# Hybrid decoder trunk: vector products of the mixer moved to GpSimd and ScalarE, one small matmul group moved by a unit

## The chip, the cores and the metric

The kernel runs on one core of a Trainium2 chip. The metric is the device time of one execution in microseconds (us), lower is better; the number compared is the median of the runs.

## The reference

The reference is a decoder trunk of two layers on 256 tokens with 1024 channels, all in float32. Each layer is a feed-forward block, a mixer and a second feed-forward block, each with an RMS norm ahead of it and added to the residual. The mixer is what the change touches:

```
h = rms_norm(x)                      # 256 x 1024
one projection h @ w_in -> columns of three causal attentions:
  A stick-breaking (4 heads)
  B NSA (8 query heads, 2 key/value groups): compressed, selected-block and sliding-window branches
      q = rope(rms_norm(q, q_norm));  k_cmp = rope(rms_norm(silu(flat @ w1) @ w2, k_norm))
  C DSA (4 query heads, one shared key head): indexer scores -> top 64 keys -> softmax
      q = rope(rms_norm(q, q_norm));  k = rope(rms_norm(k, k_norm))
merged = sum over b of sigmoid(h @ w_gate)_b * (o_b @ w_br_b);   x = x + merged @ w_out
```

Each head of 64 numbers is normed by itself: it is multiplied by its reciprocal root mean square and then by a vector of norm weights, and the first 16 numbers are rotated (rope).

## The kernel before

**Weights.** Every weight matrix is streamed from HBM in tiles `raw` of 128x1024 numbers and used in one pass. Each number is split into a high part (`wh`, rounded to the fast float32 form that TensorE takes) and the rest (`wl`): ScalarE makes `wh` by a copy (L242), VectorE makes `wl` by a subtraction (L244). One such tile with its matmuls is called a **unit** (`unit`, `run_unit`). There are three buffers for `wh` and for `wl` and four for `raw`; the split runs two units ahead of the matmuls (`LA = 2`).

**Order of the work.** TensorE's instructions stand in exactly the order of the program text: each matmul is tied behind the one before it. Around the units stand `threads`: Python generators (`keys`, `queries`, `compress`, `indexer`, `dsa`, `nsa_units` and others). After every unit `tick()` lets each thread whose wait has run out go on to its next `yield n`, which means "n units later". So a `yield` decides behind which unit a thread's matmuls stand. On the other engines a scheduler sets the order within each queue, and each queue is then run strictly in order.

**The mixer's units.** `ORDER` lists the column groups: group 0, the compressed keys' columns `f`, group 3, gate tile 0, group 4 (the NSA queries), gate tile 1, group 1 (stick-breaking), group 2, and then the ten other gate tiles. A result collects in one of three PSUM banks `acc` and must be read out ("evacuated") before the bank is used again; transposes go through two PSUM banks `tp`. `evens` (L631 on) sends evacuations to ScalarE and VectorE in turn.

**What the change touches.**
- `gate_rows` (L618 on): evacuates a finished gate bank (128x512) on VectorE, multiplied by the token norm `R`, into `gl`. The sigmoid that reads `gl` comes at the end of the mixer.
- `norm_rope` (L668 on): squares, sums, reciprocal root, product with the root (L676), product with the norm weights `hg` (L679), then `rope` (L648 to L652). It is called for the DSA heads and keys (`p1`, 9 heads) and for the two token halves of the NSA queries (`q8[0]`, `q8[1]`, 8 heads each). The page calls all of these tiles `p` or `q`.
- `keys`: splits the keys into high and low parts (`kk`, `kc`), transposes them, and evacuates the transposed DSA key as `kD` by `evens`: one token half on ScalarE (L635), the other on VectorE (L637). Then the DSA queries (`dq`, evacuated as `qD`).
- `compress`: first layer, `silu` and the second layer of the compressed keys. `hrep` is the input of the second layer and `c2s` its result; `kc` from `c2s` is transposed later and evacuated as `kC`.
- `queries`: after `norm_rope`, ScalarE makes the high part of the queries (L880) and VectorE the low part (L881).

The steps in `compress` and `queries` read:

```python
            yield 2
            c2 = hid[:, S + P:2 * S]
            for kv in range(2):
                mm(c2[:, kv * HD:(kv + 1) * HD], hrep[:, kv].rearrange("p i g c -> p (i g c)"), w2[:, kv], True, True)
...
            for t in range(NT):
                A.activation(out=q8[t][:, :, 0:HD].bitcast(F32R), in_=q8[t][:, :, HD:P], func=AF.Copy)
                V.tensor_tensor(out=q8[t][:, :, HD:P], in0=q8[t][:, :, HD:P], in1=q8[t][:, :, 0:HD], op=ALU.subtract)
```

Of the kernel before, what the change touches and what calls it, by code (L numbers as in the profile page):

```python
# [13 lines left out]
AF = mybir.ActivationFunctionType  # L14
ALU = mybir.AluOpType
AX = mybir.AxisListType

P = 128
D = 1024
S = 256  # L20
# [5 lines left out]
HD = 64  # L26
# [97 lines left out]
def decoder_trunk(ctx: ExitStack, tc: tile.TileContext, x_in, consts, gains, hgain, gu1, dn1, win, wkc, wgate, cw1, cw2,  # L124
                  cpe, wbr, wout, gu2, dn2, out, depth=DEPTH):
    nc = tc.nc
    V, A, G, T = nc.vector, nc.scalar, nc.gpsimd, nc.tensor
# [78 lines left out]
    def spawn(gen, wait=1):  # L206
        threads.append([gen, wait])
# [282 lines left out]
    def mixer(l, nrm, nxt):  # L490
# [127 lines left out]
        def gate_rows(n, a):  # L618
            def f(_):
                if a == 0:  # L620
                    return
                if n % 2 == 0:
                    gl[n // 2] = b4("gl")
                V.tensor_tensor(out=gl[n // 2][:, (n % 2) * 512:(n % 2 + 1) * 512].rearrange("p (a b) -> p a b", b=S),
                                in0=gb[n].rearrange("p (a b) -> p a b", b=S),
                                in1=N["R"].unsqueeze(1).to_broadcast([P, 2, S]), op=ALU.mult)
            return f

        turn = [0]

        def evens(out, in_):  # L631

            turn[0] ^= 1
            if turn[0]:
                A.activation(out=out, in_=in_, func=AF.Copy)  # L635
            else:
                V.tensor_copy(out=out, in_=in_)  # L637
# [28 lines left out]
        def norm_rope(v, nh, gs, t0=0):  # L666
# [10 lines left out]
            for a, n, k in gs:  # L677
                g = hg[:, k * HD:(k + 1) * HD].unsqueeze(1).unsqueeze(1)
                V.tensor_tensor(out=v[:, :, a:a + n], in0=v[:, :, a:a + n], in1=g.to_broadcast([P, nt, n, HD]),  # L679
                                op=ALU.mult)  # L680
# [91 lines left out]
        def keys():  # L772
            yield from need(0, 3)
            yield from norm_rope(p1, 9, ((0, 4, 0), (4, 1, 1), (5, 2, 2), (7, 2, 4)))
            for t in range(NT):
# [10 lines left out]
                tp = transposes([k1[:, 0, 0:P], k1[:, 0, P:256]])  # L786
                evens(out=kD[:, :, s], in_=heads(tp))
            dq = b4("dq").rearrange("p (t h a d) -> p t h a d", t=NT, a=2, d=HD)
# [14 lines left out]
        def compress():  # L803
# [36 lines left out]
            for kv in range(2):  # L840
                a, b = (v[:, kv * 2 * NC:(kv + 1) * 2 * NC].rearrange("p (g c) -> p g c", c=NC).unsqueeze(1)
                        .to_broadcast([P, 4, 2, NC]) for v in (hs, tp))
                V.tensor_tensor(out=hrep[:, kv, :, :, 0:NC], in0=b, in1=a, op=ALU.mult)
            yield 2
            c2 = hid[:, S + P:2 * S]
# [27 lines left out]
        def queries():  # L873
# [5 lines left out]
            for t in range(NT):  # L879
                A.activation(out=q8[t][:, :, 0:HD].bitcast(F32R), in_=q8[t][:, :, HD:P], func=AF.Copy)  # L880
                V.tensor_tensor(out=q8[t][:, :, HD:P], in0=q8[t][:, :, HD:P], in1=q8[t][:, :, 0:HD], op=ALU.subtract)  # L881
            yield 2
# [384 lines left out]
```

## Time and profile before

| what | value |
|---|---|
| median of 3 runs | 1208.97 us (1208.77 to 1208.98) |
| the profiled execution's own time | 1211.23 us |
| span of its trace, first to last instruction | 1209.5 us |
| TensorE busy | 1197.8 us, 99% of the span |
| VectorE busy | 884.2 us, 73% |
| ScalarE busy | 697.9 us, 58% |
| GpSimd busy | 145.8 us, 12% |
| granted TensorE clock | 1.00 in every slice, which is the 2.4 GHz level |

The engines are called PE (TensorE, its weight loads PEld), DVE (VectorE), ACT (ScalarE), POOL (GpSimd) and SP in the profile. A share over the whole span is an average over stages: the feed-forward blocks fill most of it, and the two mixers lie at about 200 to 395 us and 797 to 1000 us. Where TensorE is nearly always busy, the time follows from the few places where it isn't, and from what ends the wait there.

### The profile page before, as it was taken

The page shows a single profiled execution, that of the slowest core. Times are in us where ns is not written, and L with a number is a line of the kernel's source. Part 1 is how long each engine was busy: PE and PEld are TensorE (multiplying, and loading weights), DVE is VectorE, ACT ScalarE, POOL GpSimd, SP SyncE. Part 2 cuts the span into 40 slices and gives each one's busy share as a digit, 9 for nine tenths or more (in the row PEclk, how much of TensorE's full clock was granted, in tenths as well). Part 3 has the DMA queues.
Part 4 walks back from the last instruction along what each step waited for, and adds up shares of the span by engine and source line. Part 5 has one row for each costly group of instructions (what it writes and reads, how often), then busy time and mean ns, then how long its engine had stood idle before and what let it go on. Part 6 is the DMA issues. An engine that isn't in the chain of part 4 may idle for free. (4 is left out here: it accounts for less than half of the span.)

```text
span 1209.5 us, 20859 instructions
## 1 busy us (share of the span) xinstructions
PE 1197.8 (99%) x7878; PEld 1070.7 (89%) x7878; DVE 884.2 (73%) x1577; ACT 697.9 (58%) x1261; POOL 145.8 (12%) x181
## 2 busy tenths in 40 slices
PE   8999999999999999999999999999999999999998
PEld 7888888879999988888888888898898999888887
DVE  7766677897766877776777666788977587876664
ACT  6655555565675565555555555555666745655542
POOL 2211011220000111110111110112100001111100
PEclk9999999999999999999999999999999999999999
DMA  7555566644334555556656555666533345555563
GB/s 263 187 185 184 179 190 200 216 152 136 122 95 152 180 189 190 190 187 190 191 181 192 189 182 184 188 188 219 166 123 113 106 155 187 191 192 192 183 200 106
DMA packets 60885, 212.09 MB, mean 175 GB/s; under 512 B 6992, under 2 KB 8048, under 8 KB 60784
## 3 DMA queue, kind: packets, MB, share of 16 engines
q1 hardware_dynamic: 60192, 209.65, 54.2%
q0 software_dynamic: 448, 1.08, 0.4%
q8 instruction: 62, 1.02, 0.3%
q14 instruction: 39, 0.32, 0.1%
q10 hardware_dynamic: 144, 0.02, 0.0%
HBM read 209.15 MB, written 1.05 MB: 174 GB/s over the span
## 5 line engine op out<-in xcount | busy, mean ns | idle before, releaser
L242 ACT ACTIVATE wh<-raw 128x1024 fp32r<-128x1024 f32 (+4 forms) x402 | 412.2, 1028 | 401.8 <-PE acc L196 277.8
L244 DVE TENSOR_TENSOR wl<-raw,wh 128x1024 fp32r<-128x1024 f32 (+4 forms) x400 | 473.9, 1187 | 211.5 <-ACT wh L242 210.6
L196 PE MATMUL acc<-aT,wh 128*128 128x512 f32 (+1 forms) x1696 | 415.1, 343 | 1.3 <-ACT wh L242 1.3
L196 PEld LDWEIGHTS acc<-aT,wh 128*128 128x128 f32 x1696 | 265.0, 189 | 41.9 <-ACT wh L242 1.7
L196 PE MATMUL acc<-aT,wl 128*128 128x256 f32 x1280 | 297.9, 281 | 1.2 <-DVE wl L244 1.2
L196 PE MATMUL acc<-hT,wh 128*128 128x512 f32 (+1 forms) x792 | 236.2, 367 | 0.0
L196 PEld LDWEIGHTS acc<-aT,wl 128*128 128x128 f32 x1280 | 216.1, 190 | 3.7 <-DVE wl L244 2.8
L196 PE MATMUL sc<-aT,wh 128*128 128x512 f32 x544 | 191.7, 396 | 0.0
L196 PE MATMUL acc<-hT,wl 128*128 128x256 f32 x704 | 184.5, 280 | 0.0
L196 PEld LDWEIGHTS acc<-hT,wh 128*128 128x128 f32 x792 | 137.2, 188 | 25.8
L196 PE MATMUL sc<-aT,wl 128*128 128x256 f32 x544 | 151.1, 279 | 0.0
L196 PEld LDWEIGHTS acc<-hT,wl 128*128 128x128 f32 x704 | 126.8, 188 | 0.0
L196 PEld LDWEIGHTS sc<-aT,wh 128*128 128x128 f32 x544 | 101.8, 188 | 24.0
L442 POOL TENSOR_TENSOR v<-v,R 128x256 f32<-128x256 f32 x88 | 70.6, 806 | 412.3 <-DVE v L358 359.2
L196 PEld LDWEIGHTS sc<-aT,wl 128*128 128x128 f32 x544 | 102.4, 188 | 0.4
L386 POOL TENSOR_TENSOR ssum<-ssum,sq 128x256 f32<-128x256 f32 x42 | 38.3, 912 | 445.5 <-ACT sq L385 445.3
L196 PE MATMUL acc<-wh,aT 128*128 128x512 f32 (+1 forms) x320 | 81.1, 394 | 0.2
L196 PEld LDWEIGHTS acc<-wh,aT 128*128 128x128 f32 x320 | 57.5, 188 | 11.0 <-ACT p L526 1.1
L357 ACT ACTIVATE half<-acc 128x256 f32<-128x256 f32 x136 | 49.5, 366 | 3.7 <-PE acc L196 3.2
L444 DVE TENSOR_TENSOR v<-v,v 128x256 f32<-128x256 f32 x88 | 38.2, 436 | 13.3 <-ACT v L443 5.8
L358 DVE TENSOR_TENSOR v<-acc,half 128x256 f32<-128x256 f32 x108 | 44.7, 417 | 1.5 <-ACT half L357 1.5
L376 DVE SCALAR_TENSOR_TENSOR aT<-x,gn,aT 128x256 fp32r<-128x256 f32 x48 | 40.6, 856 | 7.0 <-ACT aT L375 7.0
(239 smaller groups left out, 1217.2 us busy)
## 6 DMA issues: line engine op xcount, KB each, us to landing
raw<-in_gu SPq DMA_DIRECT2D x175, 512.0 KB, 4.0
raw<-in_dn SPq DMA_DIRECT2D x64, 512.0 KB, 3.7
raw<-in_wgate SPq DMA_DIRECT2D x48, 512.0 KB, 3.6
raw<-in_win SPq DMA_DIRECT2D x32, 512.0 KB, 3.7
raw<-in_dn SPq DMA_DIRECT2D x32, 384.0 KB, 3.0
raw<-in_wbr SPq DMA_DIRECT2D x16, 512.0 KB, 3.5
raw<-in_wout SPq DMA_DIRECT2D x16, 512.0 KB, 3.5
raw<-in_cw SPq DMA_DIRECT2D x8, 512.0 KB, 4.4
```

Of the source, the lines that this page charges most:

```text
L196: return pe(T.matmul(o, lhsT=lhsT, rhs=rhs, start=start, stop=stop, skip_group_check=True))
L242: A.activation(out=wh[:, w], in_=raw[:, w], func=AF.Copy)
L244: e.tensor_tensor(out=wl[:, w], in0=raw[:, w], in1=wh[:, w].bitcast(F32), op=ALU.subtract)
L357: A.activation(out=t, in_=b[:, S:2 * S], func=AF.Copy)
L358: V.tensor_tensor(out=o, in0=b[:, 0:S], in1=t, op=ALU.add)
L376: V.scalar_tensor_tensor(out=dst[:, m, 1], in0=xs[m], scalar=g[:, m:m + 1], in1=dst[:, m, 0].bitcast(F32), op0=ALU.mult, op1=ALU.subtract)
L386: G.tensor_tensor(out=ssum, in0=ssum, in1=sq, op=ALU.add)
L442: G.tensor_tensor(out=g, in0=g, in1=N["R"], op=ALU.mult)
L444: V.tensor_tensor(out=u, in0=u, in1=g, op=ALU.mult)
```

## The change

Five edits, all in the mixer, so each is made once in each of the two layers:
1. Gate tiles 0 and 1 are evacuated by ScalarE as a plain copy; their product with `R` is made by GpSimd in place, spawned for 22 units later. The ten others stay as they were.
2. The product with the norm weights goes to GpSimd for the NSA queries (8 heads); the 9 heads of `p1` stay on VectorE.
3. Both halves of `kD` are evacuated by ScalarE.
4. The second compression layer stands three units behind the first layer's last step in place of two, and what follows it in `compress` moves with it.
5. The low part of the NSA queries is made by GpSimd.

```diff
@@ gate_rows
-                V.tensor_tensor(out=gl[n // 2][:, (n % 2) * 512:(n % 2 + 1) * 512].rearrange("p (a b) -> p a b", b=S),
-                                in0=gb[n].rearrange("p (a b) -> p a b", b=S),
-                                in1=N["R"].unsqueeze(1).to_broadcast([P, 2, S]), op=ALU.mult)
+                g = gl[n // 2][:, (n % 2) * 512:(n % 2 + 1) * 512].rearrange("p (a b) -> p a b", b=S)
+                b = gb[n].rearrange("p (a b) -> p a b", b=S)
+                r = N["R"].unsqueeze(1).to_broadcast([P, 2, S])
+                if n < 2:
+
+                    A.activation(out=g, in_=b, func=AF.Copy)
+                    spawn(scaled(g, r), 22)
+                else:
+                    V.tensor_tensor(out=g, in0=b, in1=r, op=ALU.mult)
             return f
+
+        def scaled(g, r):
+            G.tensor_tensor(out=g, in0=g, in1=r, op=ALU.mult)
+            yield 1
@@ norm_rope
-                V.tensor_tensor(out=v[:, :, a:a + n], in0=v[:, :, a:a + n], in1=g.to_broadcast([P, nt, n, HD]),
+                e = G if nh == 8 else V
+                e.tensor_tensor(out=v[:, :, a:a + n], in0=v[:, :, a:a + n], in1=g.to_broadcast([P, nt, n, HD]),
                                 op=ALU.mult)
@@ keys
-                evens(out=kD[:, :, s], in_=heads(tp))
+                A.activation(out=kD[:, :, s], in_=heads(tp), func=AF.Copy)
@@ compress
-            yield 2
+            yield 3
             c2 = hid[:, S + P:2 * S]
@@ queries
-                V.tensor_tensor(out=q8[t][:, :, HD:P], in0=q8[t][:, :, HD:P], in1=q8[t][:, :, 0:HD], op=ALU.subtract)
+                G.tensor_tensor(out=q8[t][:, :, HD:P], in0=q8[t][:, :, HD:P], in1=q8[t][:, :, 0:HD], op=ALU.subtract)
```

**The order on each engine.** The rows below are of the first layer; the second layer's read alike. A tile's last number is its buffer. Line numbers of the changed kernel are some 10 higher from `norm_rope` on.

ScalarE, from the evacuation of the second half of the window and selected keys (`kSW`) to the evacuation of group 1 (`p` from `acc_2930`), before:

```order
L784 ACTIVATE kSW_2164<-tp_2950 128x4x128
L242 ACTIVATE wh_3001<-raw_2999 128x1024
L699 ACTIVATE kc_564_2878<-c2s_2752 128x128
L880 ACTIVATE q_402_2153<-q_402_2153 128x8x64
L242 ACTIVATE wh_3029<-raw_3027 128x1024
L795 ACTIVATE qD_2163<-tp_3017 128x4x128
L869 ACTIVATE kC_2166<-tp_3023 128x64
L880 ACTIVATE q_403_2154<-q_403_2154 128x8x64
L242 ACTIVATE wh_3068<-raw_3066 128x1024
L526 ACTIVATE p_406_2157<-acc_2930,rq_2149 128x256
L526 ACTIVATE p_406_2157<-acc_2930,y_2224 128x256
```

The same place after the change:

```order
L795 ACTIVATE kSW_2164<-tp_2950 128x4x128
L891 ACTIVATE q_402_2153<-q_402_2153 128x8x64
L242 ACTIVATE wh_3001<-raw_2999 128x1024
L710 ACTIVATE kc_569_2919<-c2s_2806 128x128
L798 ACTIVATE kD_2165<-tp_2986 128x2x128
L891 ACTIVATE q_403_2154<-q_403_2154 128x8x64
L242 ACTIVATE wh_3025<-raw_3023 128x1024
L806 ACTIVATE qD_2163<-tp_3017 128x4x128
L242 ACTIVATE wh_3068<-raw_3066 128x1024
L526 ACTIVATE p_406_2157<-acc_2930,rq_2149 128x256
L526 ACTIVATE p_406_2157<-acc_2930,y_2224 128x256
```

The first high part of the queries (`q_402`) has moved ahead of `wh_3001` and `kc`; `kD` has come in behind them, and `kC` stands behind the evacuations of group 1 now.

GpSimd, from the low part of the DSA queries (`dq`) on, before:

```order
L790 TENSOR_TENSOR dq_2990<-p_401_2152,dq_2990 128x8x64
L865 TENSOR_TENSOR p_565_2881<-c2s_2752,cst 128x512
L700 TENSOR_TENSOR kc_564_2878<-c2s_2752,kc_564_2878 128x128
L244 TENSOR_TENSOR wl_3184<-raw_3181,wh_3183 128x1024
L386 TENSOR_TENSOR ssum_146<-ssum_146,sq_4759 128x256
```

And after the change:

```order
L801 TENSOR_TENSOR dq_2990<-p_401_2152,dq_2990 128x8x64
L876 TENSOR_TENSOR p_570_2922<-c2s_2806,cst 128x512
L636 TENSOR_TENSOR gl_2620<-gl_2620,R_2334 128x512
L690 TENSOR_TENSOR q_402_2153<-q_402_2153,hg_2139 128x8x64
L690 TENSOR_TENSOR q_403_2154<-q_403_2154,hg_2139 128x8x64
L892 TENSOR_TENSOR q_402_2153<-q_402_2153 128x8x64
L711 TENSOR_TENSOR kc_569_2919<-c2s_2806,kc_569_2919 128x128
L892 TENSOR_TENSOR q_403_2154<-q_403_2154 128x8x64
L244 TENSOR_TENSOR wl_3184<-raw_3181,wh_3183 128x1024
```

Five products of 512 columns have come between; the gate product (L636) stands here and not 22 units on, and the one of gate tile 0 stands ahead of the first `kk`.

TensorE, at the transposes of the DSA queries (`dq`) and of the compressed key (`kc`), before:

```order
L689 MATMUL tp_2986<-cst,kc_563_2865 128x128 x2
...
L689 MATMUL tp_3017<-cst,dq_2990 128x128 x4
L689 MATMUL tp_3023<-cst,kc_564_2878 128x128 x2
...
L689 MATMUL tp_3050<-cst,dq_2990 128x128 x4
L196 MATMUL acc_3072<-wh_3001,aT_143 128x512 x2
```

And after the change:

```order
L700 MATMUL tp_2986<-cst,kc_561_2853 128x128 x2
...
L700 MATMUL tp_3017<-cst,dq_2990 128x128 x4
...
L700 MATMUL tp_3046<-cst,dq_2990 128x128 x4
L700 MATMUL tp_3062<-cst,kc_569_2919 128x128 x2
L196 MATMUL acc_3072<-wh_3001,aT_143 128x512 x2
```

Between two of these rows that are parted by "..." stands one unit. The compressed key's transposes stand a unit later, and the third user of a `tp` bank, which needs the bank of `kD` (`tp_2986`), is a unit further from it.

## Rows read from the trace of the kernel before

**Rows 1.** The page: busy time, share of the span, instructions of each engine.
```profile
PE 1197.8 (99%) x7878; PEld 1070.7 (89%) x7878; DVE 884.2 (73%) x1577; ACT 697.9 (58%) x1261; POOL 145.8 (12%) x181
```

**Rows 2.** TensorE's waits: who for whom, us in total, times, longest.
```profile
PE tp L689 <- DVE kD L637: 2.9, 2, 1.5
```

**Rows 3.** Busy us of each engine in one stretch of either mixer.
```profile
246.00:267.00 21.00, 19.77 (x123) 17.33 (x122) 21.00 (x65) 12.29 (x27) 5.86 (x5) 1.00 0.41 126
843.40:864.40 21.00, 19.74 (x123) 17.28 (x122) 21.00 (x66) 12.33 (x27) 5.85 (x5) 1.00 0.41 126
```

**Rows 4.** Timeline of TensorE, first mixer: start, us, instruction, idle before and releaser.
```profile
245.68 0.63 PE L196 MATMUL o<-w,hrep 128*128 128x64 f32 x4 [0.70 <-ACT wh L242]
...
265.17 0.60 PE L689 MATMUL tp<-cst,dq 128*128 128x128 f32 x4
267.24 0.41 PE L689 MATMUL tp<-cst,kc 128*128 128x128 f32 x2 [1.47 <-DVE kD L637]
267.40 2.08 PE L196 MATMUL acc<-wh,aT 128*128 128x512 f32 x8
...
270.24 0.60 PE L689 MATMUL tp<-cst,dq 128*128 128x128 f32 x4
270.59 2.48 PE L196 MATMUL acc<-wh,aT 128*128 128x512 f32 x8
```

**Rows 5.** Timeline of VectorE, first mixer.
```profile
235.55 0.68 DVE L624 TENSOR_TENSOR gl<-acc,R 128x512 f32<-128x512 f32 x1
...
258.62 0.67 DVE L624 TENSOR_TENSOR gl<-acc,R 128x512 f32<-128x512 f32 x1
...
261.12 0.40 DVE L758 MATCH_REPLACE8 isc<-m,isc 128x256 f32<-128x256 f32 x1
...
262.64 0.68 DVE L679 TENSOR_TENSOR q<-q,hg 128x512 f32<-128x512 f32 x1
...
264.34 0.95 DVE L679 TENSOR_TENSOR q<-q,hg 128x512 f32<-128x512 f32 x1
...
266.48 0.28 DVE L652 TENSOR_TENSOR q<-ra,rb 128x128 f32<-128x128 f32 x1
266.68 0.41 DVE L637 CAST kD<-tp 128x256 fp32r<-128x256 f32 x1
```

**Rows 6.** Timeline of ScalarE, first mixer.
```profile
263.49 0.31 ACT L699 ACTIVATE kc<-c2s 128x128 fp32r<-128x128 f32 x1 [0.96 <-DVE y L663]
266.79 0.63 ACT L880 ACTIVATE q<-q 128x512 fp32r<-128x512 f32 x1 [2.99 <-DVE q L652]
267.33 1.04 ACT L242 ACTIVATE wh<-raw 128x1024 fp32r<-128x1024 f32 x1
268.27 0.58 ACT L795 ACTIVATE qD<-tp 128x512 fp32r<-128x512 f32 x1
268.75 0.21 ACT L869 ACTIVATE kC<-tp 128x64 fp32r<-128x64 f32 x1
...
270.54 0.46 ACT L526 ACTIVATE p<-acc,rq 128x256 f32<-128x256 f32 x1
270.89 0.47 ACT L526 ACTIVATE p<-acc,y 128x256 f32<-128x256 f32 x1
```

**Rows 7.** Timeline of GpSimd and VectorE where both work, first mixer.
```profile
242.87 0.48 DVE L748 SCALAR_TENSOR_TENSOR isc<-rl,iw,isc 128x256 f32<-128x256 f32 x1
243.18 1.33 POOL L700 TENSOR_TENSOR kk<-p,kk 128x512 f32<-128x512 f32 x1 [20.19 <-ACT kk L699]
243.71 1.08 DVE L748 SCALAR_TENSOR_TENSOR isc<-rl,iw,isc 128x256 f32<-128x256 f32 x1
...
255.24 2.18 POOL L790 TENSOR_TENSOR dq<-p,dq 128x512 f32<-128x512 f32 x1
256.26 1.26 DVE L657 TENSOR_SCALAR u<-hs 128x8 f32<-128x8 f32 x2
257.50 1.05 POOL L865 TENSOR_TENSOR p<-c2s,cst 128x512 f32<-128x512 f32 x1
```

## The prediction

> **What bounds the kernel now.** I read the page first, then TensorE's waits, then one stretch of each mixer, and in it the timelines of the four engines. TensorE is busy 99% of the span [rows 1], so only the places where it stands still can give time back, and all of them together are 1209.5 - 1197.8 = 11.7 us. The largest wait that recurs is that of a transpose for `kD`: 2.9 us in two times, once in each mixer [rows 2]. In that stretch VectorE is busy 21.00 us of 21.00, in the second mixer as in the first, while TensorE loses 1.2 us by this count [rows 3]. So here VectorE's queue sets the pace.
>
> TensorE's timeline shows the wait itself. The DSA query transposes start at 265.17, the compressed key's at 267.24 after an idle 1.47, the next unit at 267.40 [rows 4]. Without a wait these transposes take 0.35 (270.24 to 270.59) and the key's 0.16 (267.24 to 267.40), so the unit would begin at 265.68: the wait costs 1.72 us by start times, 1.47 by the modelled end. In the first mixer the second compression layer adds 0.70 [rows 4]; the other mixer does not have it.
>
> What TensorE waits for is `kD` on VectorE at 266.68, which stands in its queue right behind the end of the first query rope (L652, 266.48 + 0.28 = 266.76) [rows 5]. ScalarE waits for the same event: its `q` (L880) starts at 266.79 after an idle 2.99 [rows 6]. I call the end of this first rope X; before it is 266.76. Everything below is a question of when X comes and what ScalarE has to do after it.
>
> **What is removed.** Edits 3 and 4 take away the wait for `kD` on VectorE and put a unit between the transposes that share its bank; edit 4 takes away the 0.70. Were nothing to take their place, TensorE would gain 2 x 1.72 + 0.70 = 4.1 us. That is the ceiling.
>
> **When X comes without contention.** Ahead of X, VectorE's queue loses the two gate products (0.68, 0.67) and both products with the norm weights (0.68, 0.95), and the order puts one match-replace of 0.40 behind X [rows 5]. That is 3.38 us of durations; neighbours in the queue overlap by some 0.08 each, so 3.0 of queue time. X would be 266.76 - 3.0 = 263.8. The product with the norm weights lies on the way, by GpSimd: 1.05 to 1.33 for 512 columns [rows 7]. Behind the product with the root VectorE still has the other half's product with its root and a weight subtraction ahead of the rope, so GpSimd's latency is covered; uncovered it would cost 0.4 to 0.65 more than VectorE's 0.68.
>
> **What GpSimd's products cost VectorE.** Two engines at work are not two engines at full speed here. While GpSimd ran `kk` from 243.18 to 244.51, a score step of VectorE took 1.08 where its neighbour of the same shape took 0.48: 0.60 lost. While `dq` ran, two steps of 8 columns took 1.26, which should be over in about 0.2: 1.04 lost; and `dq` itself took 2.18 where `kk`, of the same size, took 1.33 [rows 7]. So a GpSimd product of 512 columns costs VectorE between nothing (where its next steps do not collide) and 1.04. After the change three such products stand in front of X: that of gate tile 1 and the two with the norm weights, with a weight subtraction and the rope waiting right behind the last two. They are nearest to the `dq` case. I take 0.9 each, 2.7 in all: X = 266.5. The bounds are 263.8, and with a fourth collision (the `p` product of 1.05 [rows 7], which now falls among small products) and 1.04 each, 267.9. The first gate product comes in a stretch where I count neither loss nor gain beyond its 0.68.
>
> The Trainium skill's page "SBUF — State Buffer", section "SBUF: two separate sides", speaks against this change. It says that GpSimd and a VectorE instruction with two SBUF inputs share one pair of ports under an exclusive lock, and that the second to issue is blocked until the first has finished. The trace agrees in kind: the `dq` row and its neighbours show blocking in both directions. By the rule to the letter each of the three products would cost its whole 1.05 to 1.33 rather than my 0.9, and the sum would end nearer to the slower rival below.
>
> **What ScalarE has to do after X.** Before, between X and the moment at which the first bank of group 1 is free again (second evacuation, 270.89 + 0.47 = 271.36 [rows 6]) lie 4.60 us. TensorE needs that bank for the third matmul of the next group's first unit: that unit's 8 matmuls take 2.48 where the unit ahead of it takes 2.08 [rows 4], so already now this is a near thing. After the change the order puts the first `q` in front of `wh_3001`, and that with `kc` and `kD` behind it, so all of these come after X. By start-to-start times of [rows 6]: `q` 0.54, `wh` 0.94, `kc` 0.2, `kD` 0.3 (estimate, between `kC` 0.21 and `qD` 0.58), `q` 0.54, `wh` 0.94, `qD` 0.48, `wh` 0.94, two evacuations 0.82. That is 5.70, or 1.1 more than before. The bank is free at X + 5.70; break-even is X = 265.66.
>
> With X = 266.5 the bank is free at 272.2, that is 0.84 us later than before. TensorE arrives there at about 268.5 if nothing stops it (270.59 - 1.72 - 0.70, and 0.4 for two matmuls), so it waits for some 3.7 us, spread over two places: about 0.8 at the second group of DSA query transposes, which now need the bank of `kD` evacuated by ScalarE at X + 2.0, and the rest at the third matmul of group 2. So the removed 1.72 and 0.70 are paid back, and 0.84 more. The stretch of the second mixer reads like the first [rows 3], so twice: **+1.7 us**.
>
> **Edits that I cost at nothing.** The two gate evacuations on ScalarE (0.58 by the `qD` row of 128x512 from PSUM [rows 6]) lie ahead of ScalarE's idle 2.99 before X; without this cover they would cost 0.5 each. The low parts of the queries leave VectorE behind X; their readers are transposes two units on, so neither 0.68 twice less on VectorE nor GpSimd's 1.3 shows, unless they hold the second rope (below). Gate products in `gl` are read at the end of the mixer. No DMA moves; the rest of the program keeps its order.
>
> **The sum.** The profiled execution's span is 1209.5 us and its own time 1211.23, 2.3 above the median; I apply the difference to the median: 1208.97 + 1.7 = **1210.7 us**. A measurement of this kernel can tell a change of about 0.2%, 2.4 us, from none, so this is within it. This case holds as long as X lies between 264.5 and 266.8 (1.2 us per mixer on either side of break-even): 1206.6 to 1211.4, chance 0.42.
>
> **Rival 1: the collisions mostly miss, faster.** Match-replaces, maxima and steps that read PSUM may fill the time of GpSimd's products; [rows 7] show that some steps pass beside one. Then X is 263.8 to 264.4, the bank is free at 269.5 to 270.1, and each mixer gains 1.9 to 1.3: 1205.3 to 1206.5. Against it speaks that VectorE's queue has no idle time there and that the weight subtraction, two inputs from SBUF, comes right behind. Chance 0.25.
>
> **Rival 2: each product blocks in full, slower.** Place: VectorE's queue between the second root product and X, then ScalarE's second `q`. With 1.2 us lost at each of the three products, between the 1.05 and the 1.33 of [rows 7], X is 267.4, the bank is free at 273.1, 1.74 later than before; if the low part of the first half then holds the second rope by another 0.5, 2.2. Twice that gives 1212.4 to 1213.4. It decides from X = 266.86 on. That is the rule of the Trainium skill's page named above, taken literally; the `dq` row's 2.18 supports it, the `kk` row's loss of 0.60 doesn't. Chance 0.33.
>
> **Rival 3: an edit does not do what it says.** The gate products are spawned for 22 units later, but the scheduler's order has them at once: that of gate tile 1 right ahead of the products with the norm weights. Were they to run late as written, X would be 0.9 earlier, 265.6, and the sum zero: 1209.0. The order excludes it; it is part of the first case.
>
> **How the numbers follow.** Faster by over 0.2% is rival 1, 0.25; slower by over 0.2% rival 2, 0.33; within it the forecast, 0.42. The range takes in both rivals to their near ends and most of their length, 1205.6 to 1213.0.
>
> **What will show it.** Right: TensorE's wait for `kD` on VectorE and that for the second compression layer are gone; the transposes of the second DSA query group wait for ScalarE; group 2's first unit takes 4 us or more in place of 2.48; ScalarE stands idle well over the 2.99 ahead of the first `q`; steps of VectorE beside the new GpSimd products are stretched by about 0.9; X lies at 266 to 267 on the old scale. Wrong, to the fast side: X before 264.5 and the first unit of group 2 near 3 us. Wrong, to the slow side: X past 267, or a new wait of TensorE for `wl` in the units around the DSA queries, whose subtractions stand between GpSimd's products.

## The result and the profile after

The changed kernel takes **1219.14 us** (median of 4 runs, 1218.02 to 1220.18) where the kernel before takes 1208.87 on the same chip (4 runs): ratio 1.0089, 95% interval 1.0076 to 1.0101. The forecast was 1210.7 and the range ended at 1213.0, so the change costs about 10 us where I had it at 1.7.

Whole executions of one kernel differ by up to 5 us (the kernel before: 1205.9 to 1210.6 on one chip). A part of that lies far from the change: in the profiled execution of before, TensorE's work is 1.9 us later than in that of the changed kernel by the time the first mixer begins. So the two mixers are also compared by themselves, by the start of the same TensorE instruction in both traces:

| start in before | 237.82 | 279.69 | 842.06 | 883.17 |
|---|---|---|---|---|
| start in the changed kernel | 235.88 | 281.02 | 843.47 | 889.97 |
| difference | -1.94 | +1.33 | +1.41 | +6.80 |

The first mixer costs 1.33 + 1.94 = 3.27 us, the second 6.80 - 1.41 = 5.39, and in between nothing changes: 8.7 us, the idle times and the lower clock around the transposes of the DSA queries and the compressed key. The trace of before is of an execution at 1211.23 us, above every other execution of that kernel on record (1205.9 to 1210.6), so differences against it flatter the changed kernels: in every row of the table below the medians differ by 0.9 to 3.8 us more than the two mixers together. Two variants compare better in this way than a variant and before. Below, "mixer 1" and "mixer 2" are these two differences. The old scale of the prediction's times is the changed kernel's plus 1.94.

TensorE's waits in the changed kernel (who for whom, us in total, times, longest):

```profile
PE tp L700 <- ACT qD L806: 3.2, 2, 1.6
PE tp L700 <- ACT kD L798: 2.2, 2, 1.1
PE acc L196 <- DVE wl L244: 1.8, 5, 0.5
PE acc L196 <- ACT p L526: 1.5, 2, 0.8
```

The wait for `kD` on VectorE [rows 2] and that for the second compression layer [rows 4] are gone. Three waits for ScalarE, once in each mixer, have taken their place. TensorE's timeline in the first mixer shows them in a row:

```profile
263.10 2.08 PE L196 MATMUL acc<-wh,aT 128*128 128x512 f32 x8
...
267.21 0.66 PE L700 MATMUL tp<-cst,dq 128*128 128x128 f32 x4 [1.12 <-ACT kD L798]
269.45 0.44 PE L700 MATMUL tp<-cst,kc 128*128 128x128 f32 x2 [1.58 <-ACT qD L806]
269.64 0.71 PE L196 MATMUL acc<-wh,aT 128*128 128x512 f32 x2
271.12 2.75 PE L196 MATMUL acc<-wh,aT 128*128 128x512 f32 x6 [0.77 <-ACT p L526]
273.67 1.59 PE L196 MATMUL acc<-wl,aT 128*128 128x512 f32 x4
```

Together they are 3.47 us in place of 1.47 and 0.70 [rows 4]. The last two rows show something else: six matmuls with 512 columns take 2.75 us where eight took 2.08, and no wait is in them. The view by stretches has the reason. Its columns are the stretch, its length, the busy us of PE, PEld, DVE, ACT and POOL with their counts, the granted clock, the DMA share and GB/s; four stretches are of the first mixer, four of the second:

```profile
268.00:270.00 2.00, 0.55 (x4) 0.47 (x4) 2.00 (x7) 2.00 (x3) 1.96 (x1) 1.00 0.10 10
270.00:272.00 2.00, 1.23 (x5) 0.69 (x4) 2.00 (x7) 2.00 (x6) 0.10 (x1) 0.84 0.79 250
272.00:274.00 2.00, 2.00 (x6) 1.63 (x5) 1.97 (x7) 0.49 (x3) 0.00 (x0) 0.50 0.56 129
274.00:276.00 2.00, 2.00 (x8) 1.59 (x8) 1.28 (x2) 0.97 (x1) 0.00 (x0) 0.81 0.70 184
...
872.00:874.00 2.00, 1.31 (x3) 1.11 (x4) 2.00 (x7) 1.97 (x6) 0.00 (x0) 0.52 0.58 221
874.00:876.00 2.00, 2.00 (x6) 1.52 (x6) 1.97 (x6) 0.34 (x1) 0.00 (x0) 0.50 0.75 207
876.00:878.00 2.00, 2.00 (x7) 1.52 (x6) 0.79 (x2) 0.71 (x1) 0.00 (x0) 0.50 0.45 104
878.00:880.00 2.00, 2.00 (x8) 1.62 (x7) 0.65 (x1) 0.00 (x1) 0.00 (x0) 0.77 0.80 248
```

Behind the cluster of idle times the granted clock falls to 0.50, the 1.2 GHz level. What a stretch at a lower clock leaves undone is its length by the share that is missing: 2.00 x (0.16 + 0.50 + 0.19) = 1.70 us in the first mixer, 2.00 x (0.48 + 0.50 + 0.50 + 0.23) = 3.42 in the second. This is an upper estimate, since in the second mixer some 0.6 us of the slow stretch are a wait in any case. So up to 5.1 of the 8.7 us are the clock's, and 3.5 (1.57 and 1.97) are left for the queues, where I had 0.84 twice.

ScalarE's queue shows the other half, as foreseen. In its timeline the first `q` waits for the end of the rope (7.37 idle, 2.99 in [rows 6]), and everything that TensorE needs stands behind it:

```profile
265.11 0.63 ACT L891 ACTIVATE q<-q 128x512 fp32r<-128x512 f32 x1 [7.37 <-DVE q L662]
265.65 1.04 ACT L242 ACTIVATE wh<-raw 128x1024 fp32r<-128x1024 f32 x1
...
266.79 0.36 ACT L798 ACTIVATE kD<-tp 128x256 fp32r<-128x256 f32 x1
267.33 0.63 ACT L891 ACTIVATE q<-q 128x512 fp32r<-128x512 f32 x1 [0.17 <-DVE q L662]
267.87 1.04 ACT L242 ACTIVATE wh<-raw 128x1024 fp32r<-128x1024 f32 x1
268.81 0.58 ACT L806 ACTIVATE qD<-tp 128x512 fp32r<-128x512 f32 x1
...
270.60 0.47 ACT L526 ACTIVATE p<-acc,y 128x256 f32<-128x256 f32 x1
```

Why the rope is late stands in VectorE's timeline, in some of its steps with two inputs:

```profile
232.89 2.67 DVE L690 TENSOR_TENSOR p<-p,hg 128x512 f32<-128x512 f32 x4
...
256.57 1.08 DVE L673 SCALAR_TENSOR_TENSOR y<-w,y 128x8 f32<-128x8 f32 x2
...
259.25 1.27 DVE L673 SCALAR_TENSOR_TENSOR y<-w,y 128x1 f32<-128x1 f32 x1
...
261.58 1.30 DVE L866 SCALAR_TENSOR_TENSOR c2s<-c2s,y,hg 128x64 f32<-128x64 f32 x1
...
264.74 0.28 DVE L662 TENSOR_TENSOR q<-ra,rb 128x128 f32<-128x128 f32 x1
...
266.02 1.22 DVE L662 TENSOR_TENSOR q<-ra,rb 128x128 f32<-128x128 f32 x1
```

GpSimd's timeline has the four products of 512 columns that lie beside them, and the first low part:

```profile
233.23 1.52 POOL L636 TENSOR_TENSOR gl<-gl,R 128x512 f32<-128x512 f32 x1 [12.17 <-ACT gl L629]
...
256.24 1.31 POOL L636 TENSOR_TENSOR gl<-gl,R 128x512 f32<-128x512 f32 x1
...
258.73 4.07 POOL L690 TENSOR_TENSOR q<-q,hg 128x512 f32<-128x512 f32 x2 [1.18 <-DVE w L672]
265.82 1.27 POOL L892 TENSOR_TENSOR q<-q 128x512 f32<-128x512 f32 x1 [3.02 <-ACT q L891]
```

Beside each GpSimd product some step of VectorE lasts about a microsecond too long: the four products at 232.89 take 2.67 in place of 1.56, the two steps at 256.57 take 1.08 in place of 0.23 (both e12, below), the step of one column at 259.25 takes 1.27 and that of 64 columns at 261.58 takes 1.30, which are 0.15 and 0.27 in e1, and the end of the second rope takes 1.22 where that of the first takes 0.28. The first rope, X, ends at 265.02, that is 266.96 on the old scale.

### The profile page after: what moved, and what is told of

The parts are those of the page before. It is cut to its first block, busy times and chain, and to the rows that moved or that the text cites. A ratio compares the mean times of both kernels' runs of the same rounds, so it can differ in the third digit from the quotient of the medians.

```text
span 1216.2 us, 20875 instructions
## 1 busy us (share of the span) xinstructions
PE 1201.1 (99%) x7878; PEld 1073.6 (88%) x7878; DVE 887.7 (73%) x1563; ACT 699.6 (58%) x1267; POOL 165.0 (14%) x193
## 3 DMA queue, kind: packets, MB, share of 16 engines
q0 software_dynamic: 448, 1.08, 0.4%
q8 instruction: 62, 1.02, 0.4%
## 4 chain that ended last, share of the span: by engine, by line
PE 92%; DVE 5%; ACT 1%; issue 1%; DMA 0%; POOL 0%; DVEq 0%; ACTq 0%; POOLq 0%
PE acc L196 71%; PE sc L196 17%; PE tp L700 2%; DVE wl L244 2%; PE o L196 2%; ACT wh L242 1%; DVE isc L769 0%; PE tp L196 0%; DMA gn<-in_gains 0%; DVE y L673 0%; DVE m L768 0%; DVE isc L759 0%; DVE hs L683 0%; DVE aT L376 0%; ACT aT L375 0%
## 5 line engine op out<-in xcount | busy, mean ns | idle before, releaser
L196 PE MATMUL acc<-wh,aT 128*128 128x512 f32 (+1 forms) x320 | 84.2, 406 | 1.5 <-ACT p L526 1.5
```

Source lines behind the costliest of these rows:

```text
L196: return pe(T.matmul(o, lhsT=lhsT, rhs=rhs, start=start, stop=stop, skip_group_check=True))
```

## The experiments

The theory has three links: (a) each GpSimd product takes about 0.9 from VectorE, whoever waits for its result, so the rope is late; (b) ScalarE's queue behind the rope turns this into waits of TensorE; (c) the waits take the granted clock down, which costs several microseconds on top. The rivals: ScalarE's order or its new evacuations alone; waiting for GpSimd's results and not its work; a clock that has nothing to do with the waits. Edits are numbered as in the section on the change. "Idle" is the sum of TensorE's idle times from 0.2 us on in the stretch, "clock" the time lost at a granted clock under 1.00, worked out as above; both, like the mixers, are of the one profiled execution, while median, before and ratio are of all runs on the same chip.

| kernel | median | before | ratio (95%) | mixer 1 | mixer 2 | idle 1, 2 | clock 1, 2 |
|---|---|---|---|---|---|---|---|
| changed | 1219.14 | 1208.87 | 1.0089 (1.0076 to 1.0101) | +3.27 | +5.39 | 3.8, 3.7 | 1.7, 3.4 |
| e1: edits 3, 4 | 1208.11 | 1208.69 | 0.9994 (0.9985 to 1.0004) | -1.87 | -0.50 | 0.8, 1.1 | 0, 0 |
| e2: all but 2 | 1211.74 | 1208.69 | 1.0025 (1.0015 to 1.0035) | +0.02 | +0.42 | 2.4, 1.9 | 0, 0 |
| e3: changed + fill | 1215.02 | 1208.69 | 1.0052 (1.0035 to 1.0068) | +1.80 | +3.63 | 1.7, 2.7 | 0, 0 |
| e4: `q` behind `kD` | 1218.26 | 1208.69 | 1.0082 (1.0067 to 1.0097) | +2.93 | +3.41 | 3.9, 3.2 | 1.7, 1.7 |
| e5: e1 + unused products | 1210.80 | 1207.31 | 1.0021 (1.0010 to 1.0031) | -0.13 | +0.36 | 2.2, 1.8 | 0, 0 |
| e6: edits 3, 4, 5 | 1207.97 | 1207.31 | 1.0004 (0.9994 to 1.0013) | -1.33 | -0.96 | 1.1, 0.8 | 0, 0 |
| e7: edits 1, 3, 4 | 1209.43 | 1207.31 | 1.0016 (1.0006 to 1.0026) | -0.28 | +0.09 | 2.1, 1.5 | 0, 0 |
| e8: e1 + tie | 1205.68 | 1207.31 | 0.9986 (0.9977 to 0.9994) | -2.33 | -1.54 | 0.3, 0 | 0, 0 |
| e9: edits 2, 3, 4 | 1210.31 | 1207.83 | 1.0019 (1.0010 to 1.0029) | -0.86 | +1.80 | 1.8, 1.9 | 0, 1.7 |
| e10: all but 1 | 1211.04 | 1207.83 | 1.0024 (1.0014 to 1.0035) | -0.75 | +0.12 | 1.7, 1.6 | 0, 0 |
| e11: all but 5 | 1215.79 | 1207.83 | 1.0062 (1.0047 to 1.0077) | +1.89 | +3.22 | 2.9, 3.1 | 1.7, 1.7 |
| e12: gate products late | 1211.50 | 1207.64 | 1.0031 (1.0022 to 1.0041) | +1.22 | +0.91 | 2.3, 2.4 | 1.7, 0 |

**e1, edits 3 and 4 alone.** Against the kernel before:

```diff
-                evens(out=kD[:, :, s], in_=heads(tp))
+                A.activation(out=kD[:, :, s], in_=heads(tp), func=AF.Copy)
...
-            yield 2
+            yield 3
```

Expected: 

> The kernel before with the key's second evacuation on ScalarE and the second compression layer a unit later, and none of the work moved to GpSimd. Theory (GpSimd's products hold VectorE's rope back, ScalarE's queue behind it turns that into waits of TensorE, and the cluster of these waits takes the granted clock down): no new GpSimd product, so the first rope ends at 266.8 on the old scale, but the order now has wh_3001, the key and kD in front of the first query copy on ScalarE, so TensorE waits neither for kD nor for the second layer; each mixer gains 1 to 2 us, 1205 to 1207, with the granted clock at 1.00 throughout the stretch. Rival A (the evacuations put on ScalarE are themselves what costs, GpSimd has no part): the waits for ScalarE's kD and qD and the clock at the lower level stay, 1213 or more. Rival B (nothing is to be had here, the unit later only moves the stall): 1208 to 1210.

Rival A falls: with both evacuations on ScalarE the clock stays at 1.00. By start times 2.4 us are gained, as the theory had it; the median, 0.6 under before, misses the forecast, lies where rival B has it and is too little to tell. The first rope ends at 264.42, that is 264.57 on the old scale, 2.2 earlier than the 266.8 that I expected. Of the 4.1 of the ceiling, 1.5 are lost again to one new wait: TensorE's third matmul of group 2 waits 0.78 in each mixer for `p`.

**e2, the products with the norm weights back on VectorE.** Against the changed kernel:

```diff
-                e = G if nh == 8 else V
-                e.tensor_tensor(out=v[:, :, a:a + n], in0=v[:, :, a:a + n], in1=g.to_broadcast([P, nt, n, HD]),
+                V.tensor_tensor(out=v[:, :, a:a + n], in0=v[:, :, a:a + n], in1=g.to_broadcast([P, nt, n, HD]),
```

Expected: 

> The changed kernel with the two products with the norm weights back on VectorE (gates, low parts, kD and the later layer as changed). Theory: of the three products that hold the rope only that of gate tile 1 is left, the rope ends about 1 us earlier or as late, and the order has wh_3001 ahead of the first query copy on ScalarE; TensorE's waits for kD and qD on ScalarE shrink below 1 us together and the granted clock stays up: 1206 to 1210. Rival A (the order on ScalarE alone matters): the same direction, but the rope is no earlier than 266.8 on the old scale. Rival B (low parts or gates are the cause): no better than the changed kernel, 1217 or more.

The clock stays up and most of the loss is gone, but the median is outside what I expected, and TensorE has a wait of 1.15 that I hadn't seen coming. It is for the key's low part on GpSimd, which stands there behind the first low part of the queries, and that takes 2.60 in place of 1.3. The first rope ends at 265.99 on the old scale, 1.0 earlier than in the changed kernel, as expected, so rival A falls.

**e3, the idle times filled.** Ahead of the second group of DSA query transposes, and of the compressed key's, in the changed kernel:

```diff
+FILL = 20
...
+                if t == 1:
+                    fb = psum("sc", SC)
+                    for _ in range(FILL):
+                        mm(fb[:, 0:P], warm, warm, True, True)
...
+            fb = psum("sc", SC)
+            for _ in range(FILL):
+                mm(fb[:, 0:P], warm, warm, True, True)
```

Expected: 

> The changed kernel with 20 more 128x128 matmuls, results unused, in each of the two places where TensorE stands idle (ahead of the second group of DSA query transposes and ahead of the compressed key's transposes). They add work to the kernel; nothing else is moved. Theory (the lower clock is the result of the idle times and costs about 1.7 us in the first mixer and 3.2 in the second): the granted clock stays at 1.00 in the stretch, the waits for VectorE and ScalarE stay as long as they are since the fill stands within them, and the kernel takes 1213 to 1216, faster than the changed one in spite of the added work. Rival (the clock falls for some other reason, or the time lost in it would be lost to the waits anyway): 1219 to 1222.

The same stretches as above, in this kernel:

```profile
272.00:274.00 2.00, 1.22 (x5) 0.86 (x5) 2.00 (x8) 2.00 (x6) 0.00 (x0) 1.00 0.70 238
...
874.00:876.00 2.00, 1.79 (x8) 1.50 (x9) 2.00 (x7) 1.58 (x6) 0.00 (x0) 1.00 0.43 156
```

80 matmuls more, 4.1 us less than the changed kernel. With TensorE at work through the two first waits the granted clock stays at 1.00 in both mixers, and no other engine's order changes. That shows link (c). By start times the gain is 3.2 and not 5.1: 5.1 was an upper estimate, the fill isn't free, and in the second mixer a wait for `wl` is 1.41 where the changed kernel has 0.28.

**e4, the query copies behind `kD` on ScalarE.** A tie of order alone, against the changed kernel; the scheduler answered it with moves of its own, of one step of the top-64 search on VectorE and of the key's low part on GpSimd:

```diff
-                A.activation(out=kD[:, :, s], in_=heads(tp), func=AF.Copy)
+                mark[0] = A.activation(out=kD[:, :, s], in_=heads(tp), func=AF.Copy)
...
-                A.activation(out=q8[t][:, :, 0:HD].bitcast(F32R), in_=q8[t][:, :, HD:P], func=AF.Copy)
+                nosync(A.activation(out=q8[t][:, :, 0:HD].bitcast(F32R), in_=q8[t][:, :, HD:P], func=AF.Copy), mark[0])
```

Expected: 

> The changed kernel with one tie of order alone: the two high-part copies of the queries stand behind both evacuations of kD on ScalarE, so its order there is wh_3001, key, kD, q, q, wh, qD in place of q, wh_3001, key, kD, q, wh, qD. All of GpSimd's products stay. Theory: wh_3001, the key and kD no longer wait for the rope; TensorE's wait of 1.12 for kD goes, that for qD (1.58) and for the first bank of group 2 stays and may grow by what is left of ScalarE's queue behind the rope (q, q, wh, qD 2.5 us); with one idle less the clock may stay up: 1212 to 1217. Rival (ScalarE's order is the whole matter, GpSimd's products cost nothing): 1206 to 1209. Rival (the products alone matter, the order nothing): 1218 to 1220.

I missed: 1218.26. TensorE's timeline has one wait in place of two, and it is as long as both:

```profile
268.29 0.60 PE L700 MATMUL tp<-cst,dq 128*128 128x128 f32 x4
272.01 0.53 PE L700 MATMUL tp<-cst,kc 128*128 128x128 f32 x2 [3.12 <-ACT qD L807]
```

ScalarE's order only decides at which transposes TensorE waits for the late rope, and one idle of 3.12 takes the clock down (0.56 from 272 to 274) as the cluster does. So the rival that order is the whole matter falls too, and the other one, the products alone (1218 to 1220), has the time right.

**e5, GpSimd products that nobody needs.** Against e1, in `norm_rope`; no other engine's order differs from e1's:

```diff
+DUM = 1
...
+            for x in range(DUM if nh == 8 else 0):
+                x = OT[0][:, 0:2].rearrange("p a s -> p (a s)").rearrange("p (a b c) -> p a b c", a=1, b=nh)
+                y = r.unsqueeze(3).to_broadcast([P, nt, nh, HD])
+                G.tensor_tensor(out=x, in0=y, in1=y, op=ALU.mult)
```

Expected: 

> The kernel of e1_o34 with two more products of 512 columns on GpSimd in each mixer, beside VectorE's own products with the norm weights; they read a small tile that VectorE has just written, their result is used by nobody, and the order of instructions on every other engine is that of e1_o34. Theory (GpSimd's products cost VectorE time by themselves, whatever waits for their result): VectorE's steps beside them are stretched by 0.9 to 1.2 each, the first rope ends 1.8 to 2.4 later than the 264.42 of e1_o34, TensorE's wait for the first bank of group 2 grows from 0.78 to some 2.5, and the kernel takes 1211 to 1214, more if the granted clock falls. Rival (what costs in the changed kernel is only that VectorE's next step waits for GpSimd's result): nobody waits here, so within 0.5 of e1_o34.

VectorE's timeline in the first mixer:

```profile
257.11 0.54 DVE L664 SCALAR_TENSOR_TENSOR y<-w,y 128x8 f32<-128x8 f32 x1
...
258.25 0.99 DVE L663 SCALAR_TENSOR_TENSOR w<-w,u 128x1 f32<-128x1 f32 x1
```

And GpSimd's, with the two products:

```profile
256.59 1.04 POOL L681 TENSOR_TENSOR iqS<-y 128x512 fp32r<-128x512 f32 x1 [0.65 <-DVE w L663]
257.80 1.43 POOL L681 TENSOR_TENSOR iqS<-y 128x512 fp32r<-128x512 f32 x1 [0.17 <-DVE w L662]
```

Both steps take 0.15 in e1. Here the first ends at 257.65, GpSimd's product at 257.63; the second at 259.24, the product at 259.23. VectorE's two root products are 0.89 and 1.73 later against TensorE's work than in e1, and the kernel loses 1.7 and 0.9 us in its mixers. Nobody waits for the result: link (a) holds, at 0.84 to 0.89 for a product. The median, 1210.80, is just under the range that I expected and well over the rival's. The Trainium skill's page "SBUF — State Buffer", section "SBUF: two separate sides", says that a GpSimd instruction and a VectorE one with two SBUF inputs exclude each other on a shared pair of ports; that VectorE's steps end with GpSimd's product agrees. What I got wrong is where TensorE then waits: for `wl` (1.16 and 0.74), not longer for the first bank.

**e6, e7 and e9, one more edit each on top of e1**: the low parts, the gate tiles, the norm weights. Against e1:

```diff
@@ queries, e6
-                V.tensor_tensor(out=q8[t][:, :, HD:P], in0=q8[t][:, :, HD:P], in1=q8[t][:, :, 0:HD], op=ALU.subtract)
+                G.tensor_tensor(out=q8[t][:, :, HD:P], in0=q8[t][:, :, HD:P], in1=q8[t][:, :, 0:HD], op=ALU.subtract)
@@ gate_rows, e7
+                if n < 2:
+
+                    A.activation(out=g, in_=b, func=AF.Copy)
+                    spawn(scaled(g, r), 22)
...
@@ norm_rope, e9
-                V.tensor_tensor(out=v[:, :, a:a + n], in0=v[:, :, a:a + n], in1=g.to_broadcast([P, nt, n, HD]),
+                e = G if nh == 8 else V
+                e.tensor_tensor(out=v[:, :, a:a + n], in0=v[:, :, a:a + n], in1=g.to_broadcast([P, nt, n, HD]),
```

Expected of e6: 

> The kernel of e1_o34 with the low parts of the queries on GpSimd as well. Theory: they stand behind the key's low part in GpSimd's queue here, not ahead of it, and behind the first rope; VectorE loses two products of 0.67 and has match-replaces stretched beside them. 1207 to 1210. Rival (these products hold the key's low part and the second rope, and are what made e2_no2 slower than e1_o34 by 3.6): 1210 to 1212.

Expected of e7: 

> The kernel of e1_o34 with the two gate tiles evacuated by ScalarE and multiplied by GpSimd as well. Theory: VectorE is rid of two products of 0.68 and is stretched by about 0.9 beside the second of GpSimd's, in front of the rope, so the rope ends about as early or late as in e1_o34 (264.0 to 265.0), but the order on ScalarE then has both query copies together ahead of the next weight split: 1207 to 1210. Rival (the gate edit is a gain that the others hide): 1204 to 1206.

Expected of e9: 

> The kernel of e1_o34 with the two products with the norm weights on GpSimd as well (no gates, no low parts). Theory: VectorE is rid of two products of 0.68 but is stretched by 0.85 to 1.2 beside each on GpSimd, so the first rope ends 0.5 to 1.5 later than in e1_o34, and the order has the first query copy ahead of the key and kD on ScalarE; TensorE waits for kD, qD and the first bank of group 2 by 2 to 2.5 together in each mixer, where it was 1.1, and the granted clock stays at 1.00 or nearly: 1209.5 to 1212. Rival (these two products alone bring the fall of the clock and most of the loss of the changed kernel): 1214 to 1218.

All three times came out as the theory had them; that the clock falls in one mixer of e9, it had not. By start times the low parts cost 0.1 us here, the gate tiles 2.2, the norm weights 3.3. In e9 the two mixers tell the clock's price once more. They have nearly the same waits (1.02 and 0.77, 1.17 and 0.77), but the granted clock falls in the second alone, and the six matmuls behind the wait for `p` take 1.65 and 2.34:

```profile
268.66 1.65 PE L196 MATMUL acc<-wh,aT 128*128 128x512 f32 x6 [0.77 <-ACT p L526]
...
866.32 2.34 PE L196 MATMUL acc<-wh,aT 128*128 128x512 f32 x6 [0.77 <-ACT p L526]
```

**e10 and e11, the changed kernel without edit 1 and without edit 5.** The gate tiles, or the low parts, are back on VectorE:

```diff
@@ gate_rows, e10
-                if n < 2:
-
-                    A.activation(out=g, in_=b, func=AF.Copy)
-                    spawn(scaled(g, r), 22)
...
@@ queries, e11
-                G.tensor_tensor(out=q8[t][:, :, HD:P], in0=q8[t][:, :, HD:P], in1=q8[t][:, :, 0:HD], op=ALU.subtract)
+                V.tensor_tensor(out=q8[t][:, :, HD:P], in0=q8[t][:, :, HD:P], in1=q8[t][:, :, 0:HD], op=ALU.subtract)
```

Expected of e10: 

> The changed kernel with the two gate tiles evacuated and multiplied by VectorE, as before. Theory: wh_3001 is ahead of the first query copy on ScalarE again and one of GpSimd's three products in front of the rope is gone, so TensorE's waits in each mixer come to 2 to 3 us in place of 3.5; whether that lowers the granted clock is open: 1210 to 1213 if not, 1214 to 1217 if it does. Rival (the gate edit only relieves VectorE): slower than the changed kernel, over 1220.

Expected of e11: 

> The changed kernel with the low parts of the queries back on VectorE. Theory: the second rope is no longer held by a product of GpSimd (1.22 in place of 0.28 in the changed kernel), so the second group of query evacuations comes about 0.9 earlier and TensorE's wait of 1.58 for it shrinks to about 0.7; the waits come to 2.5 in each mixer: 1213 to 1217, the lower end if the granted clock stays at 1.00. Rival (the low parts cost nothing, as in e6_o345): 1218 to 1220.

By start times, the whole loss is gone without the gate edit, and in the profiled execution the clock stays up. By the medians 3.2 us of the 10.3 are left, and the clock is not up in all executions of e10: over the whole span five of the ten have 0.997 or 0.998 (1211.0 to 1213.7 us), as the profiled e9 and e12 have with one fall each (0.998), and the others 0.999 or 1.00 (1208.8 to 1211.1). Without the low parts 3.5 us are gone, 1.7 of them the clock's in the second mixer; TensorE's wait for the second query group shrinks from 1.58 to 1.29 and not to 0.7 as expected. In e6 the same low parts cost nothing. What they cost seems to come where the second rope is still ahead, as in the changed kernel, where its last step takes 1.22 beside the first of them.

**e12, the gate products behind both ropes.** A tie of order on GpSimd; every other engine's order is that of the changed kernel:

```diff
-            G.tensor_tensor(out=g, in0=g, in1=r, op=ALU.mult)
+            nosync(G.tensor_tensor(out=g, in0=g, in1=r, op=ALU.mult), low[0])
...
-                G.tensor_tensor(out=q8[t][:, :, HD:P], in0=q8[t][:, :, HD:P], in1=q8[t][:, :, 0:HD], op=ALU.subtract)
+                low[0] = G.tensor_tensor(out=q8[t][:, :, HD:P], in0=q8[t][:, :, HD:P], in1=q8[t][:, :, 0:HD], op=ALU.subtract)
```

Expected: 

> The changed kernel with one tie of order on GpSimd alone: the two gate products stand behind the low part of the second query half, so behind both ropes; the order of every other engine is that of the changed kernel. Theory (each product of 512 columns on GpSimd in front of the rope makes it 0.85 to 1 later): the first rope ends about 0.9 earlier against TensorE's work, the waits in each mixer fall from 3.5 to about 2.5: 1217 if the granted clock falls as in the changed kernel, 1212 to 1214 if it stays at 1.00. The prediction's third rival gives for this case 0.9 earlier and a sum of nothing, 1209. Rival (ScalarE's queue and the evacuations decide, not GpSimd): within 0.5 of the changed kernel, 1218.5 to 1220.

7.6 us less than the changed kernel by the medians, 6.4 when each is taken against before on its own chip; a little under what I expected, from the place of two GpSimd instructions in each mixer. VectorE's rows that answer to those above:

```profile
232.39 1.56 DVE L692 TENSOR_TENSOR p<-p,hg 128x512 f32<-128x512 f32 x4
...
255.41 0.23 DVE L675 SCALAR_TENSOR_TENSOR y<-w,y 128x8 f32<-128x8 f32 x2
...
262.72 0.28 DVE L664 TENSOR_TENSOR q<-ra,rb 128x128 f32<-128x128 f32 x1
```

The four products of the 9 heads take 1.56 in place of 2.67: that was the first gate product, 1.1. The steps at 255.41 take 0.23 in place of 1.08: that was the second, 0.85. The rope ends at 263.00 in place of 265.02, at the same pace of TensorE (0.06 apart at the mixer's start). VectorE is 0.50 behind e12 ahead of the first gate product, 1.62 behind it, 1.16 ahead of the second and 2.02 at the rope's end. So both gate products count, 0.7 to 1.1 and 0.85, though the first runs 30 us ahead of the rope: VectorE is busy 32.97 us of the 33 from 232 to 265 and has no idle time in which to lose its delay.

**e8, a version that beats both.** e1 with the weights' high part (`wh_3068`) behind the evacuations of group 1 on ScalarE:

```diff
-            A.activation(out=wh[:, w], in_=raw[:, w], func=AF.Copy)
+            i = A.activation(out=wh[:, w], in_=raw[:, w], func=AF.Copy)
+            if pre:
+                nosync(i, pev[0])
```

`pre` is set for the third unit behind group 1, `pev[0]` is the second evacuation of its first bank; on VectorE the low part of the same weights moves back with it. Expected: 

> The kernel of e1_o34 with one order-only tie: on ScalarE the high part of the weights two units on stands behind the evacuations of group 1 instead of ahead of them. In e1_o34 TensorE waits 0.78 in each mixer for the second evacuation of the first bank, which stands behind that 1.05 of work; the split weights are not needed for another 4 us. Theory: the wait goes, in both mixers, 1.5 us less than e1_o34: 1205 to 1207 by the median of the same chip, with no new wait. Rival (the wait moves to the weights' low part on VectorE): as e1_o34.

TensorE's third matmul no longer waits:

```profile
268.39 2.18 PE L196 MATMUL acc<-wh,aT 128*128 128x512 f32 x8
```

3.9 of the 4.1 us of the ceiling are there by start times, but the median is only 1.6 us (0.14%) under the kernel before.

## Why the prediction was wrong

**The place: right. The ceiling: right for one trace.** The outcome was decided at X and in ScalarE's queue behind it, and by start times e8 has 3.9 of the 4.1. But the trace of before has something of its own in the first mixer. Rows of its ScalarE and VectorE:

```profile
236.66 1.06 ACT L242 ACTIVATE wh<-raw 128x1024 fp32r<-128x1024 f32 x1 [2.41 <-DMA raw<-in_win]
238.24 0.35 DVE L746 TENSOR_SCALAR isc<-rl,iw 128x256 f32<-128x256 f32 x1 [1.14 <-ACT rl L742]
...
245.31 0.27 DVE L843 TENSOR_TENSOR hrep<-o,hs 128x120 f32<-128x120 f32 x1
```

A tile of weights was late in this one execution: in e1, whose order on ScalarE is that of before up to here, the same instruction waits 0.52 for it (at 234.18). VectorE stood idle 1.14 for it, and from there its queue is full up to `hrep`, which ends at 245.58; TensorE's second compression layer, with its 0.70, starts at 245.68. The second mixer has neither idle time at this place. So the 0.70 is not shown to be edit 4's gain in other executions, and the median of e8 shows 1.6 of the 4.1.

**X: 266.5 forecast, 266.96 measured, near by luck.** The price of a GpSimd product, 0.9, was about right: 0.84 to 0.89 in e5, 1.11 and 0.85 for the gate products and, by the steps at 259.25 and 261.58, 1.12 and 1.03 for the two with the norm weights. Wrong was the sentence that the first gate product comes in a stretch where I count neither loss nor gain: 0.7 to 1.1 of it reaches X. So four products cost X 3.7 to 4.1, where I had 2.7 for three. The time without contention was wrong the other way: 266.96 less these is 262.9 to 263.3, not 263.8. VectorE's idle 1.14 above is in the 266.76 of before and not in the changed kernel, which would explain it, and e1, with nothing moved to GpSimd, has X 2.2 earlier than before, where I had counted 0.4; no run shows it by itself.

**ScalarE after X: 5.70 forecast, 6.05 measured** (265.02 to 271.07). With X that makes the bank free 1.65 later than before, not 0.84, and the first mixer loses 1.57 without the clock. The sum of TensorE's three waits came out (3.5 for 3.7). Their places did not: I had the rest at the third matmul and overlooked that the compressed key's transposes, moved there by edit 4, need the bank that `qD` leaves (1.58).

**The step that failed: the sum took TensorE to lose only what it waits.** The 3.7 us of waits that I forecast in one place stood in the text, and what they do to the clock did not: up to 5.1 of the 8.7 us by start times, and 4.1 by the medians of e3. In before, a single idle of 1.47 [rows 4] leaves the clock at 1.00, and I read no further. Without the 5.1 the profiled execution, 1218.02, would be at 1212.9, at the end of the range. All that I named as signs of being right came true, and of those of being wrong only small waits for `wl` (0.34 and 0.28); none of the signs was about the clock. Smaller parts of the miss are the queues, 3.5 in place of 1.7, and the 1.6 us by which the medians differ more than the mixers.

**The costs at nothing.** The gate evacuations and products cost 2.2 alone (e7). The low parts were put at nothing unless they hold the second rope; they do hold it, and e11 is 3.5 us better off without them by start times, 1.7 of it the clock's.

**The rivals.** Rival 1 is out: no product missed. Rival 2's outcome, without the clock, is what happened (bank 1.65 later, it had 1.74; X past its 266.86), but by four products of 0.85 to 1.12 each and not by three of 1.2. The rule that it rested on, of the Trainium skill's page "SBUF — State Buffer", section "SBUF: two separate sides", was right in kind, as e5 shows; the loss is under a product's whole time, 1.04 and 1.43 there, where VectorE is in another step when the product starts. Rival 3's condition was made true in e12: X came 2.0 earlier than in the changed kernel, not 0.9, and the kernel was still 0.31% slower than before, with the clock down in one mixer.

**What stays open.** Which idle times take the clock down isn't settled: 2.3 us in two pieces did in e12's first mixer, 2.4 in its second did not, nor did 2.4 in e2; in e9 1.9 did and 1.8 did not, and in e10 executions of one kernel differ. Why it stayed down twice as long in the changed kernel's second mixer isn't settled either, nor the 1.9 us by which executions differ ahead of the first mixer, nor why the trace of before is 2.3 us above its median beyond the late tile.

## What to carry to other kernels

Moving work from a full VectorE to an idle GpSimd is no gain while the two block each other: here VectorE was rid of 0.68 per 512 columns and lost 0.84 to 1.12, a delay that its queue carries along until it next stands idle. So put such work behind the step that others wait for, by an explicit tie if a scheduler would hoist it (e12: 7.6 us for two instructions, though it is still 0.31% slower than before). Before counting gains on a trace, see whether its execution is a typical one: here it was 2.3 us above the median, and a late tile of weights passed for a wait that the edit would remove. When a forecast puts several microseconds of TensorE's waits close together, price the lower clock too, and test it by filling the gap with unused matmuls.

## What the runs showed of the hardware that I had not expected

Unused matmuls in a wait made the kernel 4.1 us faster (e3): the clock that they kept up was worth more than the time they took. And the blocking goes the other way for longer. In e1, beside VectorE's back-to-back steps with two inputs (two weight subtractions and the ropes, 263.01 to 266.03), a GpSimd product of 128 columns, which takes 0.47 to 0.86 us in before, lasted 3.26, as GpSimd's timeline of e1 has it:

```profile
263.09 3.26 POOL L700 TENSOR_TENSOR kc<-c2s,kc 128x128 f32<-128x128 f32 x1 [6.08 <-ACT kc L699]
```
